# Background modulations of a two-layer decoder trunk: the sum over partitions with ones as weights, and a row that goes through DRAM

## The chip, the cores and the metric

The kernel runs on one core of one Trainium2 chip. The metric is the device time of one execution in microseconds (us): the median of three runs, with the lowest and the highest beside it. Engines are named as in the profile: PE is TensorE (PEld its weight loads), DVE is VectorE, ACT is ScalarE, POOL is GpSimd. SP only issues DMAs here, one after the other, and a DMA that has to wait holds back all that stand behind it on SP.

## The reference

The trunk has two layers of two sub-layers each, numbered j = 0 to 3 below: a gated spatial mixer (0), a squared-ReLU MLP (1), dilated attention (2) and a second MLP (3). Each sub-layer is modulated by one conditioning vector:

```python
def ada_mod(c, w, b):
    m = jax.nn.silu(c) @ w + b
    shift, scale, gate = jnp.split(m, 3, axis=-1)
    return shift[:, None, :], scale[:, None, :], 1.0 + gate[:, None, :]
...
for i in range(DEPTH):
    shift, scale, gate = ada_mod(c, ada_w[i, 0], ada_b[i, 0])
    h = x * (1.0 + scale) + shift
    y = mixer_a(h, ...) if i % 2 == 0 else mixer_b(h, ...)
    x = layer_norm(ALPHA * x + gate * y, ln_g[i, 0], ln_b[i, 0])
    shift, scale, gate = ada_mod(c, ada_w[i, 1], ada_b[i, 1])
    h = x * (1.0 + scale) + shift
    x = layer_norm(ALPHA * x + gate * squared_relu_mlp(h, ...), ln_g[i, 1], ln_b[i, 1])
```

x is 1024 rows of 1024 features, c one row of 1024, and each w is 1024 x 3072, all in float32. The change concerns `silu(c) @ w + b` alone: for each j three rows of 1024 numbers.

## The kernel before

All large products run on PE as three passes of a high and a low part ("hi" and "lo", made by `split`, L112: ACT copies, DVE subtracts). The work goes through the stages mixer (`mixer_a`), first MLP (`mlp(1)`), values, attention, second MLP (`mlp(3)`). A scheduler sets each engine's order from the order of the program and its own estimate of times; instructions marked `keep_in_program_order` stay where the program has them.

The modulations of j = 0 are made at the start. The others are **background work**: `ada_steps` (L133) cuts them into small steps, `later` (L199) puts the steps into one queue, and `tick` (L206) takes the next step from it at fixed places of the foreground: in the mixer two at a time or six per weight unit (L634, L661, L704), in the first half of an MLP one or two per product (L992). A group is one half row of 512 numbers (half h of part 0, shift, 1, scale, or 2, gate). Its steps are:

- eight steps (L142): load 128 x 512 of w (L145, tile `adaw`, four buffers), multiply by silu(c), which lies along the partitions, and add to the accumulator `adaacc` (DVE, L148 and L151). After eight steps the sum over the 128 partitions is still to be taken.
- `reduce` (L159): split `adaacc` into `adahi` and `adalo`.
- `total` (L168), held back until the third step of the next group is queued: the sum over partitions on PE. For a gate (part 2) the ones are the weights and the 512 columns stream past them (L173, L174), so that every partition of the bank `psa` holds the whole row; DVE adds 1 (L176) and one partition is written to `gate_dram` (L177). For shift and scale, which are needed with features along the partitions, `mod_cols` (L122) has the parts as weights, 128 columns at a time, and streams two columns of ones (L126, L127): eight weight loads and eight matmuls of 128x2. DVE adds the bias from the bank (L131). When both shift and scale of a half are there, three more DVE instructions (L185 to L187) fold them with the layer norm's weights into `mul` and `add`.

The banks of `psa` come from the PSUM pool `tr`, which has two buffers and also serves the mixer's transposes (`pszt`, L716). There are 12 groups of shift and scale in the background: four for j = 1 in the mixer, four for j = 2 and four for j = 3 in `mlp(1)`; and eight of gates.

In the mixer the names that matter are: `u_unit` (L694) with its weights `winu_hi` and `winu_lo` (units u0 to u7; four buffers each, so u4 takes the tile of u0) and its sums `psu`; `norm_v` (L673), one ACT and two DVE instructions (L676 to L678) per row tile of `vz`; `part_v` (L682) with `vhi` and `vlo`; `spatial` (L686), whose matmuls `psz` (L400) read them; and `gate_unit` (L709) with the transposes `pszt` (L716) that DVE reads (L719). In an MLP's first half `left` are the weights of the products `psua`, `psub`, `psuc` (L914), made five products ahead.

Of the kernel before, what the change touches and what calls it, by code (L numbers as in the profile page):

```python
# [10 lines left out]
F32 = mybir.dt.float32  # L11
F32R = mybir.dt.float32r
AF = mybir.ActivationFunctionType
ALU = mybir.AluOpType
# [3 lines left out]
P = 128  # L18
S = 1024
D = 1024  # L20
NT = S // P
KD = D // P
HALF = 512
# [12 lines left out]
def trunk(ctx: ExitStack, tc: tile.TileContext, x, c, ada_w, ada_b, ln_g, ln_b, a_w_in, a_b_in,  # L36
# [3 lines left out]
    nc = tc.nc  # L40
    V, A, G, T = nc.vector, nc.scalar, nc.gpsimd, nc.tensor

    def pool(stack, name, bufs, **kw):
        return stack.enter_context(tc.tile_pool(name=name, bufs=bufs, reuse_waits="tile", **kw))

    cst = pool(ctx, "cst", 1)
# [7 lines left out]
    dram = pool(ctx, "dram", 1, space=DRAM)  # L54
# [10 lines left out]
    ones_r = cst.tile([P, P], F32R, name="ones_r")  # L65
# [5 lines left out]
    cols_b = cols_c[:, KD : KD + 64]  # L71
# [20 lines left out]
    def g_col(j):  # L92
        return cols[:, o_g + j * KD : o_g + (j + 1) * KD]

    def b_col(j):
        return cols[:, o_b + j * KD : o_b + (j + 1) * KD]
# [7 lines left out]
    def bank(kind, name):  # L104
        return ps[kind].tile([P, HALF], F32, name=name, tag=kind)
# [6 lines left out]
    def split(hi, lo, src, hi_engine=A, lo_engine=V):  # L112

        first = A.copy(hi, src) if hi_engine is A else hi_engine.tensor_copy(hi, src)  # L114
        return first, lo_engine.tensor_tensor(lo, src, hi, op=ALU.subtract)  # L115


    ada = [dict() for _ in range(4)]
    ada_p = vec = None
    gate_dram = dram.tile([4, D], F32, name="gate_dram")  # L120

    def mod_cols(j, part, h, pst, hi, lo):  # L122

        for k in range(4):
            w = slice(k * P, (k + 1) * P)
            T.matmul(pst[:, 2 * k : 2 * k + 2], hi[:, w], ones_r[:, 0:2], start=True, stop=False)  # L126
            T.matmul(pst[:, 2 * k : 2 * k + 2], lo[:, w], ones_r[:, 0:2], start=False, stop=True)  # L127
        src = pst[:, 0:8].rearrange("p (k t) -> p k t", t=2)[:, :, 0]
        bias = cols_b[:, 16 * j + 8 * part + 4 * h : 16 * j + 8 * part + 4 * h + 4]
        res = ada[j][part, h] = cst.tile([P, 4], F32, name=f"ada_{j}_{part}_{h}")  # L130
        V.scalar_tensor_tensor(res[:], src, float(part), bias, ALU.add, ALU.add)  # L131

    def ada_steps(j, order, raw_bufs=2):  # L133


        i, s = divmod(j, 2)
        todo = []
        for part, h in order:
            box = {}
            w0 = part * D + h * HALF  # L140

            def step(k, part=part, h=h, box=box, w0=w0):  # L142
                nm = f"{j}_{part}_{h}"
                raw = ada_p.tile([P, HALF], F32, name=f"adaw_{nm}_{k}", tag="adaw", bufs=raw_bufs)
                nc.sync.dma_start(raw[:], ada_w[i, s, k * P : (k + 1) * P, w0 : w0 + HALF])  # L145
                if k == 0:
                    acc = box["acc"] = ada_p.tile([P, HALF], F32, name=f"adaacc_{nm}", tag=f"adaacc{part % 2}")
                    ins = V.tensor_scalar(acc[:], raw[:], silu_c[:, 0:1], None, ALU.mult)  # L148
                else:
                    acc = box["acc"]  # L150
                    ins = V.scalar_tensor_tensor(acc[:], raw[:], silu_c[:, k : k + 1], acc[:], ALU.mult, ALU.add)  # L151
                tc.keep_in_program_order(ins)

            def bias_row(part=part, h=h, box=box, w0=w0):
                if part == 2:
                    row = box["row"] = ada_p.tile([P, HALF], F32, name=f"adab_{j}_{h}", tag="adaw", bufs=raw_bufs)
                    nc.sync.dma_start(row[0:1, :], ada_b[i, s, w0 : w0 + HALF].unsqueeze(0))

            def reduce(part=part, h=h, box=box):  # L159
                nm = f"{j}_{part}_{h}"  # L160
                acc = box["acc"]
                hi, lo = (ada_p.tile([P, HALF], F32R, name=f"ada{m}_{nm}", tag=f"ada{m}") for m in ("hi", "lo"))
                if part == 2:
                    V.tensor_tensor(acc[0:1, :], acc[0:1, :], box["row"][0:1, :], op=ALU.add)
                split(hi[:], lo[:], acc[:])
                box["sum"] = (hi, lo)

            def total(part=part, h=h, box=box, w0=w0):  # L168
                nm = f"{j}_{part}_{h}"
                hi, lo = box["sum"]  # L170
                pst = bank("tr", f"psa_{nm}")
                if part == 2:
                    T.matmul(pst[:], ones_r[:], hi[:], start=True, stop=False)  # L173
                    T.matmul(pst[:], ones_r[:], lo[:], start=False, stop=True)  # L174
                    row = ada_p.tile([P, HALF], F32, name=f"gaterow_{nm}", tag="gaterow")
                    V.tensor_scalar(row[:], pst[:], 1.0, None, ALU.add)  # L176
                    nc.sync.dma_start(gate_dram[j, w0 - 2 * D : w0 - 2 * D + HALF].unsqueeze(0), row[0:1, :])  # L177
                    return
                mod_cols(j, part, h, pst, hi[:], lo[:])
                if (0, h) in ada[j] and (1, h) in ada[j]:  # L180
                    sh, sc = ada[j][0, h], ada[j][1, h]
                    mul = cst.tile([P, 4], F32, name=f"mul_{j}_{h}")
                    add = cst.tile([P, 4], F32, name=f"add_{j}_{h}")
                    o = slice(4 * h, 4 * h + 4)
                    V.tensor_tensor(mul[:], g_col(j - 1)[:, o], sc[:], op=ALU.mult)  # L185
                    V.tensor_tensor(add[:], b_col(j - 1)[:, o], sc[:], op=ALU.mult)
                    V.tensor_tensor(add[:], add[:], sh[:], op=ALU.add)  # L187
                    ada[j]["mul", h], ada[j]["add", h] = mul, add

            steps = [lambda k=k, step=step: step(k) for k in range(KD)]  # L190
            todo.append(steps[:-1] + [bias_row, steps[-1], reduce, total] if part == 2 else steps + [reduce, total])
        return todo

    GATE = ((2, 0), (2, 1))
# [2 lines left out]
    background = deque()  # L197

    def later(steps):  # L199
        held = []  # L200
        for group in steps:
            background.extend(group[:3] + held + group[3:-1])
            held = group[-1:]
        background.extend([lambda: None] * 3 + held)

    def tick(n=1):  # L206
        for _ in range(n):
# [271 lines left out]
    def mixer_a():  # L479
        nonlocal ada_p, vec  # L480
        with ExitStack() as ph:
# [147 lines left out]
            for i in range(6):  # L629
                v_end(0, i)  # L630
            later(ada_steps(0, GATE, 4) + ada_steps(1, MODS + GATE, 4))
            for n, _ in enumerate(in_turn((6, 2, range(KD)))):
                if n > 1:
# [150 lines left out]
    def mlp(j, before, ahead=iter(())):  # L784
# [5 lines left out]
        if j == 1:  # L790
            later(ada_steps(2, MODS + GATE, 4) + ada_steps(3, MODS, 4))
        else:
            later(ada_steps(3, GATE, 4))
# [1197 lines left out]
```

## Time and profile before

| | us |
|---|---|
| median of 3 runs | 2668.43 (2667.54 to 2671.32) |
| profiled execution, its time | 2666.83 |
| its span in the profile | 2665.1 |
| mixer, background of j = 1 | about 85 to 245 |
| first half of `mlp(1)`, background of j = 2 and 3 | about 330 to 648 |

The profiled execution is one run of the same kernel; its own time is 1.7 us above its span, and 1.6 us below the median. Busy times of an engine are sums over its instructions; the chain of waits follows the work that ended last back from the end, and what is not on it can be lengthened without effect until it gets onto it. In the rows of the chain an engine's matmuls are shown as a start, a length and a count.

### The profile page before, as it was taken

How to read it: one execution, taken by the hardware profiler on the slowest of the kernel's cores; microseconds unless marked ns; L12 is line 12 of the kernel's file. 1: busy time of each engine (PE TensorE's matmuls, PEld its weight loads, DVE VectorE, ACT ScalarE, POOL GpSimd, SP SyncE). 2: the span in 40 equal slices, each digit the busy share in tenths (PEclk: the TensorE clock that was granted, in tenths of full speed). 3: DMA queues.
4: the chain of work that ended last, by engine and by line, in shares of the span. 5: the costliest groups of instructions: out<-in, count | busy, mean ns of one | idle time of the engine just before them, and what ended most of it. 6: DMA issues, size and time to landing. Idle time of an engine off the chain costs nothing.

```text
span 2665.1 us, 36954 instructions
## 1 busy us (share of the span) xinstructions
PE 2639.0 (99%) x13204; PEld 2184.3 (82%) x13204; DVE 1978.8 (74%) x3548; ACT 1390.0 (52%) x2623; POOL 104.4 (4%) x189
## 2 busy tenths in 40 slices
PE   8999999999999999999999999999999999999998
PEld 6788888888888888888888888888888888888887
DVE  6895798886988888555557777777658965677887
ACT  4364475555444554333436666666656655554442
POOL 0000000000000001111110000000010000000000
PEclk9999999999999999999999999999999999999999
DMA  8643357677967646565565554454783654495562
GB/s 292 191 139 99 114 183 242 227 241 265 327 208 248 205 157 214 197 205 182 182 204 152 158 134 131 136 148 136 227 230 123 220 178 158 146 318 191 178 208 89
DMA packets 335068, 505.28 MB, mean 190 GB/s; under 512 B 51692, under 2 KB 168852, under 8 KB 334884
## 3 DMA queue, kind: packets, MB, share of 16 engines
q1 hardware_dynamic: 318500, 444.20, 52.6%
q0 software_dynamic: 16384, 58.73, 6.2%
q8 instruction: 103, 1.69, 0.3%
q14 instruction: 81, 0.66, 0.1%
HBM read 365.92 MB, written 136.92 MB: 189 GB/s over the span
## 4 chain that ended last, share of the span: by engine, by line
PE 94%; DVE 3%; DMA 1%; ACT 1%; issue 1%; SPq 0%; POOL 0%; DVEq 0%; ACTq 0%; POOLq 0%
PE psd L1081 23%; PE psua L914 13%; PE psv L1410 13%; PE psk L1511 7%; PE psuc L914 7%; PE psq L1511 7%; PE psd_wout L417 3%; PE psub L914 3%; PE pv L1684 3%; PE psv L513 3%; PE psu L701 3%; PE sc L1604 3%; PE pT L1657 1%; PE psoa L1888 1%; PE psoe L1888 1%; PE psod L1888 1%
## 5 line engine op out<-in xcount | busy, mean ns | idle before, releaser
L914 PE MATMUL psua<-right,left 128*128 128x512 f32 x1536 | 363.5, 390 | 0.1
L1081 PE MATMUL psd<-rhi,lhi 128*128 128x512 f32 x880 | 343.5, 390 | 0.0
L1081 PE MATMUL psd<-rlo,lhi 128*128 128x512 f32 x880 | 342.5, 389 | 0.0
L1081 PE MATMUL psd<-rhi,llo 128*128 128x512 f32 x880 | 342.5, 389 | 0.0
L914 PEld LDWEIGHTS psua<-right,left 128*128 128x128 f32 x1536 | 287.0, 188 | 61.3 <-DVE left L115 0.7
L1626 ACT ACTIVATE p<-p,stat 128x128 f32<-128x128 f32 (+1 forms) x384 | 168.7, 441 | 96.0 <-DVE stat L1624 92.6
L1081 PEld LDWEIGHTS psd<-rhi,lhi 128*128 128x128 f32 x880 | 165.2, 188 | 35.1 <-ACT part L945 0.9
L1081 PEld LDWEIGHTS psd<-rhi,llo 128*128 128x128 f32 x880 | 165.2, 188 | 34.6
L1081 PEld LDWEIGHTS psd<-rlo,lhi 128*128 128x128 f32 x880 | 165.2, 188 | 33.9
L914 PE MATMUL psuc<-right,left 128*128 128x512 f32 x768 | 187.2, 391 | 0.0
L914 PEld LDWEIGHTS psuc<-right,left 128*128 128x128 f32 x768 | 143.4, 188 | 30.4 <-DVE right L115 0.6
L115 DVE TENSOR_TENSOR pTlo<-pT,pThi 128x512 fp32r<-128x512 f32 (+1 forms) x160 | 99.3, 621 | 76.3 <-ACT pThi L114 75.3
L115 DVE TENSOR_TENSOR left<-ws,left 128x512 fp32r<-128x512 f32 x128 | 88.0, 689 | 81.0 <-ACT left L114 79.3
L115 DVE TENSOR_TENSOR llo<-lraw,lhi 128x1024 fp32r<-128x1024 f32 x112 | 136.5, 1221 | 2.3 <-ACT lhi L114 2.3
L1511 PE MATMUL psk<-form_L,wqk_hi 128*128 128x512 f32 x384 | 127.1, 412 | 0.0
L1511 PE MATMUL psq<-form_L,wqk_hi 128*128 128x512 f32 x384 | 126.5, 410 | 0.0
L114 ACT CAST lhi<-lraw 128x1024 fp32r<-128x1024 f32 x112 | 116.9, 1046 | 11.7 <-PE psd L1081 6.7
L1410 PE MATMUL psv<-vrhi,form_S 128*128 128x512 f32 x384 | 119.9, 390 | 1.4 <-DVE vpart L1376 0.9
L114 ACT CAST left<-ws 128x512 fp32r<-128x512 f32 x128 | 79.2, 620 | 78.1 <-DVE ws L838 67.6
L1624 DVE CUSTOM_DVE_ANT_0 p<-sc,bias 128x128 f32<-128x128 f32 (+1 forms) x384 | 113.8, 346 | 4.8 <-PE sc L1604 4.2
L114 ACT CAST pThi<-pT 128x512 fp32r<-128x512 f32 (+1 forms) x160 | 84.7, 530 | 61.6 <-PE pT L1657 44.8
L151 DVE SCALAR_TENSOR_TENSOR adaacc<-adaw,silu_c,adaacc 128x512 f32<-128x512 f32 x140 | 105.1, 751 | 5.6 <-DMA adaw<-in_ada_w_dram 4.9
(356 smaller groups left out, 6092.6 us busy)
## 6 DMA issues: line engine op xcount, KB each, us to landing
lraw<-forms SPq DMA_DIRECT2D x112, 512.0 KB
adaw<-in_ada_w_dram SPq DMA_DIRECT2D x160, 256.0 KB
up<-in_mlp_w_up_dram SPq DMA_DIRECT2D x64, 512.0 KB
forms<-s SPq DMA_DIRECT2D x128, 256.0 KB
rraw<-in_mlp_w_down_dram SPq DMA_DIRECT2D x64, 512.0 KB
forms<-part SPq DMA_DIRECT2D x96, 256.0 KB
v<-vs POOLq DMA_DIRECT2D x48, 512.0 KB, 3.7
vraw<-in_b_w_qkv_dram SPq DMA_DIRECT2D x42, 512.0 KB
```

What stands on the lines that cost most here:

```text
L114: first = A.copy(hi, src) if hi_engine is A else hi_engine.tensor_copy(hi, src)
L115: return first, lo_engine.tensor_tensor(lo, src, hi, op=ALU.subtract)
L151: ins = V.scalar_tensor_tensor(acc[:], raw[:], silu_c[:, k : k + 1], acc[:], ALU.mult, ALU.add)
L417: T.matmul(p[:], stat[a][:, k, o : o + P], u[b][:, w], start=n == 0, stop=n == count - 1)
L513: T.matmul(sums[i][:], hT[half][a_][:, k, o : o + P], units[c, k // 2][b_][:, n : n + HALF], start=k + a_ + b_ == 0, stop=k == KD - 1 and ...
L914: T.matmul(acc, w[:, a, k, :], right[p][:, b, k, :], start=p in (1, 2, 5) and k + a + b == 0, stop=k == 3 and a == 1, skip_group_check=True)
L1081: ins = T.matmul(sums[kind, m][:], l[a][:, k, m * P : (m + 1) * P], r[b][:, k, :], start=p in (1, 5, 2, 3) and kp + k + a + b == 0, stop=k ...
L1410: T.matmul(acc, rows[:, m * P : (m + 1) * P], cols_, start=p in (1, 2, 5) and kp + k + a + b == 0, stop=kp == 1 and k == 1 and a == 1, ski ...
L1511: T.matmul(p[:], wu[a][:, k * P : (k + 1) * P], h_op(k, half, b), start=k + c_ == 0, stop=k == KD - 1 and c_ == 2)
L1624: V.tensor_tensor_reduce(out=pr, in0=banks[e][:, sl], in1=st["bias"][:, width - w :], scale=-0.125, scalar=3e38, op0=ALU.add, op1=ALU.min, ...
L1626: A.activation(pr, pr, AF.Exp, bias=nm, scale=-1.0, accum_out=l)
L1888: T.matmul(sums[i, dh][:], ending["oT"][half][a][:, k, o : o + P], ending["units"][k][b][:, w], start=k == todo[0][0] and a + b == 0, stop ...
```

## The change

`mod_cols` goes. Shift and scale now take the gates' path on PE: the ones are the weights, and `adahi` and `adalo` stream past them as 128x512, two matmuls in place of eight. The row that results is copied by ACT from the bank to SBUF (`gaterow`), one partition of it is written to a new DRAM tensor `mod_dram` by SP, and a second DMA on SP (`fetch`) reads it back so that feature k*128+p lands on partition p: 128 partitions of four numbers each, each number a 4-byte piece of its own in DRAM. DVE then adds the bias in place in SBUF (`columns`), where it added it from the bank before. `mul` and `add` are folded as before, at the second of the two parts.

`later` spreads the three: `total` stands where it stood, `fetch` goes with the next step, `columns` three steps behind that. At the end of the queue seven empty steps stand in place of three. The lines below line 130 lie 10 lines lower in the changed file.

```diff
-    def mod_cols(j, part, h, pst, hi, lo):
-        for k in range(4):
-            w = slice(k * P, (k + 1) * P)
-            T.matmul(pst[:, 2 * k : 2 * k + 2], hi[:, w], ones_r[:, 0:2], start=True, stop=False)
-            T.matmul(pst[:, 2 * k : 2 * k + 2], lo[:, w], ones_r[:, 0:2], start=False, stop=True)
-        src = pst[:, 0:8].rearrange("p (k t) -> p k t", t=2)[:, :, 0]
...
-        V.scalar_tensor_tensor(res[:], src, float(part), bias, ALU.add, ALU.add)
+    mod_dram = dram.tile([4, 2, D], F32, name="mod_dram")
...
                 pst = bank("tr", f"psa_{nm}")
+                T.matmul(pst[:], ones_r[:], hi[:], start=True, stop=False)
+                T.matmul(pst[:], ones_r[:], lo[:], start=False, stop=True)
+                row = ada_p.tile([P, HALF], F32, name=f"gaterow_{nm}", tag="gaterow")
                 if part == 2:
...
                     return
-                mod_cols(j, part, h, pst, hi[:], lo[:])
-                if (0, h) in ada[j] and (1, h) in ada[j]:
+                A.copy(row[:], pst[:])
+                nc.sync.dma_start(mod_dram[j, part, h * HALF : (h + 1) * HALF].unsqueeze(0), row[0:1, :])
+
+            def fetch(part=part, h=h):
+                if part < 2:
+                    ada[j][part, h] = cst.tile([P, 4], F32, name=f"ada_{j}_{part}_{h}")
+                    nc.sync.dma_start(ada[j][part, h][:], mod_dram[j, part, h * HALF : (h + 1) * HALF].rearrange("(k p) -> p k", p=P))
+
+            def columns(part=part, h=h):
+                if part == 2:
+                    return
+                bias = cols_b[:, 16 * j + 8 * part + 4 * h : 16 * j + 8 * part + 4 * h + 4]
+                res = ada[j][part, h][:]
+                V.scalar_tensor_tensor(res, res, float(part), bias, ALU.add, ALU.add)
+                if part == 0:
                     sh, sc = ada[j][0, h], ada[j][1, h]
...
+        nothing = lambda: None
+        held = None
+        def also(f, g):
+            return lambda: (f(), g())
+        for body, ends in steps + [([nothing] * 7, None)]:
+            if held:
+                total, fetch, columns = held
+                body = body[:3] + [total, also(fetch, body[3])] + body[4:6] + [also(columns, body[6])] + body[7:]
+            held = ends
+            background.extend(body)
```

The scheduler places neighbouring work anew around these steps. Three places are shown, all in the mixer around the second of its four groups of shift and scale (`psa_0_0`, the shift's first half for j = 1).

On ACT, before, behind the square root `r_v` of the mixer's own layer norm (the eight `vz<-vz,mv_v` are the first halves of `norm_v`):

```order
L254 ACTIVATE r_v<-r_v 128x8
L676 ACTIVATE vz<-vz,mv_v 128x512 x8
L705 ACT_TABLE_LOAD
L705 ACTIVATE ut_1195<-psu_1_1233,cols 128x512
L705 ACTIVATE ut_1295<-psu_0_1296,cols 128x512
L676 ACTIVATE vz<-vz,mv_v 128x512 x4
L114 CAST vhi_1281<-vz 128x512
```

The same place on ACT in the change:

```order
L264 ACTIVATE r_v<-r_v 128x8
L114 CAST winu_hi<-winu_raw 128x1024
L686 ACTIVATE vz<-vz,mv_v 128x512 x8
L169 COPY gaterow_0_0_1263<-psa_0_0_1260 128x512
L715 ACT_TABLE_LOAD
L715 ACTIVATE ut_1194<-psu_1_1232,cols 128x512
L715 ACTIVATE ut_1286<-psu_0_1287,cols 128x512
L686 ACTIVATE vz<-vz,mv_v 128x512 x3
L715 ACTIVATE ut_1286<-psu_1_1328,cols 128x512
L114 CAST vhi_1272<-vz 128x512
```

Two instructions have come in ahead of the first `vhi`: the cast of the weights of unit u4 (before, it stood behind the `vhi` rows) and the new copy out of `psa_0_0`.

On DVE, before, the end of the same layer norm's statistics and the beginning of `norm_v`:

```order
L259 TENSOR_TENSOR mv_v<-r_v 128x8
L671 SCALAR_TENSOR_TENSOR mv_v<-mv_v 128x8
L677 TENSOR_TENSOR vz<-vz,vg 128x512
L678 TENSOR_TENSOR vz<-vz,vb 128x512
```

And in the change, from a little earlier (`adaacc_1_1` is the background sum that runs at the time):

```order
L141 SCALAR_TENSOR_TENSOR adaacc_1_1_1226<-adaw_1_1_4_1300,silu_c,adaacc_1_1_1226 128x512
L267 TENSOR_TENSOR r_v<-r_v 128x8
L141 SCALAR_TENSOR_TENSOR adaacc_1_1_1226<-adaw_1_1_5_1315,silu_c,adaacc_1_1_1226 128x512
L268 TENSOR_SCALAR r_v<-r_v 128x8
L269 TENSOR_TENSOR mv_v<-r_v 128x8
L681 SCALAR_TENSOR_TENSOR mv_v<-mv_v 128x8
L115 TENSOR_TENSOR winu_lo<-winu_raw,winu_hi 128x1024
L687 TENSOR_TENSOR vz<-vz,vg 128x512 x2
L688 TENSOR_TENSOR vz<-vz,vb 128x512 x2
```

Three more of the background's sums (k = 3, 4 and 5 of `adaacc_1_1`, the first of them a little above these rows) and the low part of unit u4's weights now stand ahead of the first `vz<-vz,vg`; before, the three stood behind it and u4's low part far behind.

On SP, in the change, the write of the row and the read back stand directly behind each other at this place:

```order
L395 DMA winu_raw<-in_a_w_in_dram 128x8x128
L170 DMA mod_dram<-gaterow_0_0_1263 1x512
L175 DMA ada_0_0_1266<-mod_dram 128x4x1
L135 DMA adaw_0_1_2_1427<-in_ada_w_dram 128x512
L135 DMA adaw_0_1_3_1452<-in_ada_w_dram 128x512
```

Before, loads of `adaw` stood there without a break. The read waits on SP until the write has landed, and the loads behind it with it. At other groups one to five DMAs stand between the two.

More of the change, by code (lines that the diff above doesn't have):

```diff
@@ L120, in trunk @@
     gate_dram = dram.tile([4, D], F32, name="gate_dram")
-    def mod_cols(j, part, h, pst, hi, lo):
-        for k in range(4):
-            w = slice(k * P, (k + 1) * P)
-            T.matmul(pst[:, 2 * k : 2 * k + 2], hi[:, w], ones_r[:, 0:2], start=True, stop=False)
-            T.matmul(pst[:, 2 * k : 2 * k + 2], lo[:, w], ones_r[:, 0:2], start=False, stop=True)
-        src = pst[:, 0:8].rearrange("p (k t) -> p k t", t=2)[:, :, 0]
-        bias = cols_b[:, 16 * j + 8 * part + 4 * h : 16 * j + 8 * part + 4 * h + 4]
-        res = ada[j][part, h] = cst.tile([P, 4], F32, name=f"ada_{j}_{part}_{h}")
-        V.scalar_tensor_tensor(res[:], src, float(part), bias, ALU.add, ALU.add)
+    mod_dram = dram.tile([4, 2, D], F32, name="mod_dram")
     def ada_steps(j, order, raw_bufs=2):
@@ L171, in total @@
                 pst = bank("tr", f"psa_{nm}")
+                T.matmul(pst[:], ones_r[:], hi[:], start=True, stop=False)
+                T.matmul(pst[:], ones_r[:], lo[:], start=False, stop=True)
+                row = ada_p.tile([P, HALF], F32, name=f"gaterow_{nm}", tag="gaterow")
                 if part == 2:
-                    T.matmul(pst[:], ones_r[:], hi[:], start=True, stop=False)
-                    T.matmul(pst[:], ones_r[:], lo[:], start=False, stop=True)
-                    row = ada_p.tile([P, HALF], F32, name=f"gaterow_{nm}", tag="gaterow")
                     V.tensor_scalar(row[:], pst[:], 1.0, None, ALU.add)
@@ L190, in ada_steps @@
             steps = [lambda k=k, step=step: step(k) for k in range(KD)]
-            todo.append(steps[:-1] + [bias_row, steps[-1], reduce, total] if part == 2 else steps + [reduce, total])
+            todo.append((steps[:-1] + [bias_row, steps[-1], reduce] if part == 2 else steps + [reduce], (total, fetch, columns)))
         return todo
@@ L199, in later @@
     def later(steps):
[L200 to L204, printed above, removed]
+        nothing = lambda: None
[8 more added lines that the diff above has]
+            background.extend(body)
     def tick(n=1):
```

## Prediction

> **What bounds the kernel now.** I read the page's first, second and fourth parts, then the chain of waits around the background groups, then the list of who waits for whom on PE.
>
> ```profile
> span 2665.1 us, 36954 instructions
> PE 2639.0 (99%) x13204; PEld 2184.3 (82%) x13204; DVE 1978.8 (74%) x3548; ACT 1390.0 (52%) x2623; POOL 104.4 (4%) x189
> PE 94%; DVE 3%; DMA 1%; ACT 1%; issue 1%; SPq 0%; POOL 0%; DVEq 0%; ACTq 0%; POOLq 0%
> PE pszt L716 <- DVE gaterow L176: 0.8, 1, 0.8
> ```
>
> PE is busy 99% of the span and carries 94% of the chain. So a microsecond of PE in the middle is a microsecond of the kernel, as long as nobody else becomes late. The last row is the only wait of PE, of those over 0.1 us, that lies between 95 and 640 us, where the change works: in the mixer a transpose waited 0.8 us for DVE to empty a bank (`tr`, two buffers).
>
> **What a group costs on PE, before and after.** In the chain, one group of shift or scale and one group of gates, both in `mlp(1)`, with the products around them:
>
> ```profile
> 402.53 0.00 PE psa L126
> 402.53 0.11 PE psa L127
> ...
> 403.20 0.11 PE psa L127
> 403.31 2.89 PE psuc L914 x12
> 406.20 5.44 PE psua L914 x24
> ...
> 504.27 0.24 PE psa L173
> 504.51 0.24 PE psa L174
> 504.75 5.49 PE psua L914 x24
> ```
>
> Eight small matmuls take 403.31 - 402.53 = 0.78, one weight load each 0.11. The product behind them takes 2.89, where twelve matmuls take 5.44 / 2 = 2.72: another 0.17, since its first weights could not be loaded under matmuls as short as these. Together 0.95. The gate group is the form that the change gives to all: 0.24 + 0.24, and 5.49 - 5.44 = 0.05 behind it: 0.53. So each of the 12 groups saves 0.42 on PE: 5.0 us in all, 1.7 in the four groups of the mixer and 3.4 in the eight of `mlp(1)`.
>
> The Trainium skill ("TensorE: Matmul & The Clock Gate", Back-to-back issue gap) gives about 131 ns per matmul of 512 columns in a sustained stream of weight loads and matmuls; by that the pair would cost 0.26 and the 12 groups would save some 7.7 us. The trace does not agree: 0.24 for each of exactly these matmuls, and 0.227 for the products, so the sum goes by 0.24.
>
> **`mlp(1)`: what the new steps do there.** Each group adds a copy of 128x512 out of PSUM on ACT, two DMAs on SP and a wait of SP for the first of them; DVE's bias addition stays what it was (0.16 before; I take the same). The nearest rows: a copy of that shape, the write of a gate's row, and attention's write of 16 KB to DRAM with the read that waits for it, once in quiet and once in a crowded stretch.
>
> ```profile
> 400.37 0.57 ACT L919 COPY part<-psua 128x512 f32<-128x512 f32 x1
> L177 SPq DMA_DIRECT2D gate_dram<-gaterow x8: 235/246/251, 94.2 to 2146.7; - x8
> 1456.38 0.34 SPq L1717 DMA_DIRECT2D st_dram<-statT  x1
> 1457.80 1.47 SPq L1739 DMA_DIRECT2D mst<-st_dram  x3
> DMA  0030000000000016841388125671000000000000
> 1977.23 1.52 SPq L1739 DMA_DIRECT2D mst<-st_dram  x3
> 1984.09 0.17 DVE L1748 TENSOR_TENSOR mm<-mm,mst 128x16 f32<-128x16 f32 x1 [2.02 <-DMA mst<-st_dram]
> ```
>
> From issue of the write to issue of the read: 1457.80 - 1456.38 = 1.42. The digits are the DMA view of 1457 to 1462 in slices of 0.125 us: the three reads, 512 pieces of 32 bytes each, move from 1458.75 to 1460.5, so the last of them ends 1.2 after SP has issued it (1457.80 + 1.47). I take 1.5 for the write and 2 for the read. The upper end is the crowded stretch: 1984.09 less 1978.75, 5.3 for the read. The lower end is nothing for either.
>
> The Trainium skill ("DMA: Bandwidth & Descriptors", Rules for kernel authors) speaks against this read: a strided last dimension lowers to one descriptor per element and should be rearranged to be contiguous. Here that is 512 descriptors of 4 bytes; by it the read costs as many pieces as one `mst` read, whose time stands above, and no run here shows pieces of 4 bytes.
>
> After `total`, then: copy 0.6, write 1.5, issue and read 2.4, so the columns are in SBUF some 4.5 us after the matmuls, 8 in a crowd. `columns` stands four ticks, about four products of 2.72 = 10.9, behind `total`, so DVE waits little or nothing. What would wait behind it is the weights of later products:
>
> ```profile
> 410.17 0.69 DVE L115 TENSOR_TENSOR left<-up,left 128x512 fp32r<-128x512 f32 x1
> 428.75 2.89 PE psua L914 x12
> 632.49 1.22 DVE L115 TENSOR_TENSOR llo<-lraw,lhi 128x1024 fp32r<-128x1024 f32 x1
> 641.03 0.69 DVE L838 TENSOR_TENSOR s<-part,s 128x512 f32<-128x512 f32 x1 [7.32 <-ACT part L923]
> ```
>
> The first weights of the next chunk are split at 410.2 and used at 428.75, 18 us later: that is the cover, and a DVE or SP that is 3 us late costs PE nothing. The last group meets the turn to the second half of the MLP; there `columns` falls into the 7.3 us in which DVE waited anyway. So `mlp(1)` gives its 3.4 us in full. Without the cover each group would cost what the wait exceeds it by.
>
> **The mixer: what is late next.** Here DVE is the second in line, and the new order costs it time (the three pieces shown above). The rows before:
>
> ```profile
> 125.00:165.00 40.00, 40.00 (x186) 33.31 (x185) 38.31 (x73) 28.07 (x41) 0.00 (x0) 1.00 0.45 135
> 134.70 1.22 DVE L115 TENSOR_TENSOR winu_lo<-winu_raw,winu_hi 128x1024 fp32r<-128x1024 f32 x1
> 138.52 5.76 ACT L676 ACTIVATE vz<-vz,mv_v 128x512 f32<-128x512 f32 x8 [1.64 <-DVE mv_v L671]
> 139.37 0.69 DVE L677 TENSOR_TENSOR vz<-vz,vg 128x512 f32<-128x512 f32 x1 [0.88 <-ACT vz L676]
> 140.07 0.00 PE psa L126
> 144.30 1.28 ACT L705 ACT_TABLE_LOAD   x1
> 147.08 2.92 ACT L676 ACTIVATE vz<-vz,mv_v 128x512 f32<-128x512 f32 x4
> 149.91 1.65 ACT L114 CAST vhi<-vz 128x512 fp32r<-128x512 f32 x3
> 150.59 1.29 DVE L115 TENSOR_TENSOR vlo<-vz,vhi 128x512 fp32r<-128x512 f32 x2
> 151.90 1.36 PE psz L400 x6
> 158.57 1.04 ACT L114 CAST winu_hi<-winu_raw 128x1024 fp32r<-128x1024 f32 x1
> ```
>
> DVE is busy 38.3 of 40 us there, and PE takes the products `psz` at 151.90, just when `vlo` is ready. In the change the cast of u4 (158.57 before) stands ahead of the eight `vz`. It takes the buffer of u0, so it waits until PE has finished u0: 140.07 before, 139.65 with one group's saving. It ends at 140.7, so the eight end 5.76 later at 146.5, where they ended at 144.3. Then the copy 0.57, the table load 1.28, two `ut` of 0.6 (as the copy), three `vz` of 0.73 (2.92 / 4) and a third `ut`: the first `vhi` starts at 152.4 and ends at 152.9; the first `vlo` ends 0.6 later, at 153.5. PE comes to `psz` at 151.90 - 0.84 = 151.06 and needs `vlo` third, at 151.5: it **waits about 2 us**. DVE by itself says nearly the same: u4's low part ends at 140.7 + 1.2 = 141.9, sixteen `vz` of 0.6 follow (a pair takes 1.29, one 0.69), then one more, `columns`, one more, and `vlo`: 153.3 to 153.9. Bounds: nothing, if the scheduler's order meets other times; 4.5, if the read takes 5.3. I take 2, since both engines give it. `columns` itself does not wait in this sum: the copy ends at 147.1, the read is issued at about 149.3 behind the write, the columns land at 151.3, and DVE comes to them at 152.2, 2.9 after the issue. Counted in the same way, DVE comes to the first sum 3.8 and to the fourth 4.8 us after the issue of their reads; at the third it is later still.
>
> Further on the mixer's end is set by DVE either way:
>
> ```profile
> 208.14 0.68 DVE adaacc L164
> 208.82 0.61 DVE gaterow L176
> 209.48 0.66 PE pszt L716 x4
> 210.14 1.16 PE psz L400 x5
> ```
>
> This is the wait of 0.8 from the first rows: PE went on at 209.48, when DVE had emptied the gate's bank. In the change PE comes here 2 - 1.7 = 0.3 to 0.5 us later than before, and DVE, whose amount of work up to here is the same, at 208.7 to 209.5. PE therefore leaves the place between 0.5 us earlier and 0.2 later than before. Had it not waited at `psz`, it would wait here. Of the mixer's 1.7 us I count 0.2.
>
> **The sum.** -3.4 in `mlp(1)`, -0.2 in the mixer: -3.6 us. Against the profiled execution's own 2666.83 that is 2663.2; the median of the runs shown, 2668.43, is 1.6 higher, which gives **2664.8**. Behind 650 us no wait of PE has to do with the change, and the gain is carried to the end. That is 0.13%, within the 0.2% (5.3 us) that a measurement of this kernel can tell from no change.
>
> **The rivals.**
>
> - *All of it arrives.* PE saves 5.0 and the wait of 0.8 goes as well: -5.8, 2662.6, faster by more than 0.2%. For it: no wait of PE in `mlp(1)`, and only one in the mixer. Against it: DVE would have to empty the gate's bank 2 us earlier with the same work. 0.14.
> - *The columns come late in the mixer.* With 5.3 us for the read, DVE stands at the first, second and fourth sum for 5.3 less 3.8, 2.9 and 4.8: 1.5, 2.4 and 0.5 us, and PE gets this at `psz` and `pszt`: -3.6 + 4.4 = 0.8, 2669.2. For it: 256 KB loads stand ahead of the read in the same queue. Against it: the DMA share there is 0.45, not that of the crowded stretch. 0.14.
> - *SP and DVE are held up, on the other side.* One mechanism: the read of 4-byte pieces is slow in itself. Every microsecond beyond the 3.8, 2.9 and 4.8 costs DVE, and PE behind it, one at each of these sums. The gain is used up at about 5 us a read, and 0.2% slower is reached at about 7. At 8 us it is 4.2 + 5.1 + 3.2 = 12.5: -3.6 + 12.5 = +9, 2677. Against it: 512 pieces in under 2 us in quiet. 0.10.
>
> **How the numbers follow.** Forecast 0.62, the rivals 0.14, 0.14 and 0.10. The range from 2661.5 to 2670 takes in the first two rivals and about 1 us of scatter, and leaves out the third. Faster by over 0.2%: the first rival and a little of the forecast's edge, 0.17; slower 0.10; within 0.2% the rest, 0.73.
>
> **What would show it.** In the changed profile: every group of `psa` in `mlp(1)` as two rows of 0.24 and a product behind it of 2.77; PE without a wait from 330 to 648; a PE wait of about 2 us at `psz` near 151, for `vlo` or `vhi`; the wait at `pszt` near 209 smaller than 0.8; the reads landing about 2 us after their issue and no DVE idle time put down to `ada<-mod_dram` worth more than 1 us. The forecast is wrong if PE waits at `psz` by 4 or not at all, if DVE stands at `columns`, or if a product in `mlp(1)` waits for its left weights.

## The result and the profile after

| | us |
|---|---|
| before, median of 20 runs beside the change | 2669.53 (2667.54 to 2672.45) |
| the change, median of 20 runs | 2666.03 (2663.21 to 2667.99) |
| ratio, 95% interval | 0.9986 (0.9979 to 0.9992) |
| profiled execution of the change: its time, its span | 2663.68, 2662.0 |

The change is faster by 0.14%, 3.5 us in the medians; between the two profiled executions the spans differ by 2665.1 - 2662.0 = 3.1. The forecast was 3.6 less, 2664.8 from a median of 2668.43; in this timing the kernel before took 1.1 us more than that.

The page's first part, and then the list of PE's waits between 90 and 330 us (between 330 and 650 there is none):

```profile
span 2662.0 us, 36882 instructions
PE 2634.6 (99%) x13132; PEld 2180.0 (82%) x13132; DVE 1977.6 (74%) x3548; ACT 1395.4 (52%) x2635; POOL 104.4 (4%) x189
```

```profile
PE psz L410 <- ACT vhi L114: 1.9, 1, 1.9
PE psa L162 <- ACT adahi L114: 0.5, 1, 0.5
```

PE has 72 instructions fewer (12 groups of 8 matmuls became 12 of 2) and 4.4 us less work, but the span is only 3.1 shorter: a wait of 1.9 at `psz` is new, and the 0.8 at `pszt` is gone. (The 0.5 at `psa` was there before.) Where the gain lies is read from marks on PE's timeline that both kernels have: the first `psu` of the mixer, the first transpose `pst` of the mixer's output stage, the first product `psua` of `mlp(1)` and the first `psd` of its second half. Of before, then of the change (start, length, engine, line, operation):

```profile
129.03 0.62 PE L701 MATMUL psu<-hT,winu_hi 128*128 128x512 f32 x2
...
308.54 0.60 PE L820 MATMUL pst<-ident,acc 128*128 128x128 f32 x4
...
330.01 2.91 PE L914 MATMUL psua<-right,left 128*128 128x512 f32 x12
...
647.70 0.39 PE L1081 MATMUL psd<-rhi,lhi 128*128 128x512 f32 x1
```

```profile
128.91 0.62 PE L711 MATMUL psu<-hT,winu_hi 128*128 128x512 f32 x2
...
153.24 1.02 PE L410 MATMUL psz<-vhi,wsT 128*128 128x512 f32 x2 [1.87 <-ACT vhi L114]
...
308.73 0.61 PE L830 MATMUL pst<-ident,acc 128*128 128x128 f32 x4
...
330.20 2.96 PE L924 MATMUL psua<-right,left 128*128 128x512 f32 x12
...
644.57 0.39 PE L1091 MATMUL psd<-rhi,lhi 128*128 128x512 f32 x1
```

From `psua` to `psd`: 647.70 - 330.01 = 317.69 before, 644.57 - 330.20 = 314.37 now, **3.32 less**. From `psu` to `pst`: 308.54 - 129.03 = 179.51 before, 308.73 - 128.91 = 179.82 now, **0.3 more**, although three groups of the mixer lie in that stretch (the first lies ahead of it) and the wait of 0.8 went. All of the gain is made in `mlp(1)`, as far as this pair of profiles shows. These two stretches are the measure of all experiments, since the work ahead of the mixer differs from execution to execution: the first `psu` came between 128.3 and 131.1 in the profiles of this study. e1 to e7, e11 and e12 below are one execution each, so only their stretches are read, not their times.

The page's fourth part gives PE 76% of the chain and "issue" 16% in this profile; in a second profile of the same kernel it is PE 93% and issue 1%. The chain had been followed back through attention by another way, so that change of shares means nothing here.

The groups in the chain, and DVE's two waits for a read (SP's issue of the read, then the instruction of DVE that waited; between square brackets the idle time and who ended it):

```profile
402.76 0.24 PE psa L162
403.00 0.24 PE psa L163
403.24 2.77 PE psuc L924 x12
```

```profile
125.61 0.24 SPq L170 DMA_DIRECT2D mod_dram<-gaterow  x1
...
127.75 0.38 SPq L175 DMA_DIRECT2D ada<-mod_dram  x1
```

```profile
131.11 0.16 DVE L182 SCALAR_TENSOR_TENSOR ada<-ada,cols_c 128x4 f32<-128x4 f32 x1 [0.79 <-DMA ada<-mod_dram]
...
635.13 0.16 DVE L182 SCALAR_TENSOR_TENSOR ada<-ada,cols_c 128x4 f32<-128x4 f32 x1 [4.26 <-DMA ada<-mod_dram]
...
637.90 0.69 DVE L848 TENSOR_TENSOR s<-part,s 128x512 f32<-128x512 f32 x1 [2.41 <-ACT part L933]
```

A group is 0.24 + 0.24 and a product of 2.77 behind it, 0.05 over 2.72: the 0.53 of the prediction. The first read of the mixer was issued at 127.75 and DVE went on at 131.11, so it took 3.4 at most; the last of `mlp(1)`, issued at 630.91, took 4.2, and there DVE stood 4.26 us without a wait of PE.

### The profile page after: what moved, and what is told of

Same layout as the page of the kernel before. It is cut to its first block, busy times and chain, and to the rows that moved or that the text cites. A ratio compares the mean times of both kernels' runs of the same rounds, so it can differ in the third digit from the quotient of the medians.

```text
span 2662.0 us, 36882 instructions
## 1 busy us (share of the span) xinstructions
PE 2634.6 (99%) x13132; PEld 2180.0 (82%) x13132; DVE 1977.6 (74%) x3548; ACT 1395.4 (52%) x2635; POOL 104.4 (4%) x189
## 4 chain that ended last, share of the span: by engine, by line
PE 76%; issue 16%; DVE 2%; POOL 2%; DMA 2%; ACT 1%; SPq 0%; POOLq 0%; DVEq 0%; ACTq 0%
PE psd L1091 20%; PE psua L924 13%; PE psk L1521 7%; PE psuc L924 7%; PE psq L1521 6%; PE psd_wout L427 3%; PE psub L924 3%; PE pv L1694 3%; PE sc L1614 3%; PE psu L711 2%; PE psv L523 2%; PE pT L1667 1%; POOL v L1397 1%; PE psoa L1898 1%; PE psoe L1898 1%
```

## Experiments: where the gain is made

The change was split by place. In the first kernel the mixer's four groups (j = 1) keep `mod_cols`, in the second the eight of `mlp(1)` (the same with `j > 1`). `mod_cols` is the one of before; its lines are left out here:

```diff
                 pst = bank("tr", f"psa_{nm}")
+                if part < 2 and j == 1:
+                    return mod_cols(j, part, h, pst, hi[:], lo[:])
                 T.matmul(pst[:], ones_r[:], hi[:], start=True, stop=False)
...
-                if part < 2:
+                if part < 2 and not j == 1:
                     ada[j][part, h] = cst.tile([P, 4], F32, name=f"ada_{j}_{part}_{h}")
...
-                if part == 2:
+                if part == 2 or j == 1:
                     return
```

> The new form in the eight groups of mlp(1) alone, the old mod_cols in the four groups of the mixer. Theory (the whole gain is the 0.42 us a group of mlp(1)): the mixer is as before, so PE does not wait at psz near 151, waits 0.8 at pszt near 209, the product psu behind it starts at 211.3 and the transposes of the output stage at 308.7; from there to the first psd of mlp(1) it is 3.3 to 3.4 us shorter than before (644.5 instead of 647.86). Span 2661.7. Rival (the mixer's groups give their 1.7 us too): with the old form there this kernel is 1.7 slower than the change, psd first at 646.4, span 2663.7.

> The new form in the four groups of the mixer alone, the old mod_cols in mlp(1). Theory: in the mixer PE waits 1.9 at psz near 151, not at pszt near 209, and leaves the mixer 0.2 later than before; mlp(1) as before, psd first at 648.1; span 2665.3, no gain. Rival (the mixer gives 1.7 us): psd first at 646.2, span 2663.4.

The marks of `mlp(1)` in the first kernel, then in the second:

```profile
329.52 2.93 PE L948 MATMUL psua<-right,left 128*128 128x512 f32 x12
...
643.84 0.39 PE L1115 MATMUL psd<-rhi,lhi 128*128 128x512 f32 x1
```

```profile
331.91 2.90 PE L948 MATMUL psua<-right,left 128*128 128x512 f32 x12
...
649.63 0.39 PE L1115 MATMUL psd<-rhi,lhi 128*128 128x512 f32 x1
```

The stretch of `mlp(1)` was 314.32 with the new form there and 317.72 with the old. In the mixer the first kernel had no wait at `psz`, 0.8 at `pszt`, and 179.37, as before; the second had 1.6 at `psz`, none at `pszt`, and 181.10. So the halves add up: the whole gain comes from `mlp(1)`, 3.3 to 3.4 for eight groups, and the mixer gives none. The second kernel was 1.5 slower in the mixer than expected. PE's rows behind the wait are longer there, and the windows of 1 us say why (length, busy times of PE, PEld, DVE, ACT and POOL, then the granted clock, the DMA share and GB/s):

```profile
152.00:153.00 1.00, 0.00 (x0) 0.00 (x0) 1.00 (x4) 1.00 (x3) 0.00 (x0) 1.00 0.00 0
...
154.00:155.00 1.00, 1.00 (x3) 0.88 (x4) 1.00 (x4) 0.89 (x2) 0.00 (x0) 0.57 0.00 0
155.00:156.00 1.00, 1.00 (x3) 0.74 (x3) 1.00 (x3) 0.59 (x1) 0.00 (x0) 0.50 0.00 0
156.00:157.00 1.00, 1.00 (x4) 0.78 (x3) 1.00 (x2) 0.41 (x2) 0.00 (x0) 0.50 0.41 137
157.00:158.00 1.00, 1.00 (x5) 0.83 (x4) 0.86 (x2) 1.00 (x3) 0.00 (x0) 0.73 0.54 176
```

Behind its idle time PE was granted half its clock for more than 3 us. From the first `psz` to the first `pszt` it took 168.16 - 153.38 = 14.78, where the change took 166.47 - 153.24 = 13.23 at a clock of 1.00: 1.55 more. Without that the stretch is 179.55. The wait can thus cost a second time, and does so in some executions.

## Experiments: what makes vhi late in the mixer

The scheduler's new order puts two things ahead of the eight `vz`: u4's cast on ACT, which the prediction named as the cause, and three sums `adaacc` on DVE, which it did not count. Each is held back by `behind` (L107), which keeps one instruction behind another in its engine's order. First the cast, behind the last of the eight:

```diff
         ins = split(hi, lo, raw, lo_engine=lo_engine)
+        if name == "winu_4":
+            behind(ins[0], marks["vz"])
```

> The change, but the cast of u4's weights on ACT is held behind the eight vz of the first half. Theory A (the cast is what makes the eight vz and so vhi late): the eight start before 140, vhi ends about 1.5 earlier, PE's wait at psz falls from 1.9 to 0.5 or less. Theory B (the statistics mv_v, which DVE ends at 141.17, are what the eight wait for; the cast ends at 140.82): the eight still start at about 141.2, PE waits 1.9 at psz, or up to 2.6 since two other instructions of ACT have moved to between the eight and vhi. Span 2662 to 2662.6 under B.

Then the sums, behind the last instruction of the statistics `mv_v` (mean and deviation of the layer norm, which the eight `vz` need as scale and bias):

```diff
+                if (j, part, h) == (1, 1, 1) and k > 2:
+                    behind(ins, marks["mv"])
                 tc.keep_in_program_order(ins)
```

> The change, but the three sums adaacc (features 3, 4, 5 of the mixer's third group) on DVE are held behind the statistics mv_v; the scheduler then puts u4's cast behind the eight vz by itself. Theory B: mv_v ends some 2 us earlier (three sums of 0.66), near 139.2, the eight start there, PE does not wait at psz near 151 (at most 0.3). Theory of the mixer's end (DVE empties the gate's bank near 209 whatever comes before): PE waits there about 2 us instead, psu behind it starts at 211.0 to 211.5, and the span is that of the change, 2661.5 to 2662.2. Rival (the wait at psz is the whole loss): no wait of that size at pszt, psu there at 209.6, span 2660.1.

With the cast held back PE waited longer, 2.7 at `psz` and 0.5 at `pszt`, and its clock fell behind the first wait (0.81 between 156 and 162): 182.69. Without the cast the eight `vz` still could not start before 140.98, when `mv_v` ended; they started at 141.25, behind a `ut` (the copy of a `psu` out of PSUM) that the scheduler had put in the cast's place. Later a second `ut` kept ACT waiting for PE for 1.19, which made `vhi` later still. With the sums held back the wait at `psz` was 0.3, at `pszt` 0.3, and the stretch 178.70. The eight started right behind `mv_v`:

```profile
140.63 0.17 DVE L684 SCALAR_TENSOR_TENSOR mv_v<-mv_v 128x8 f32<-128x8 f32 x1
140.83 5.76 ACT L689 ACTIVATE vz<-vz,mv_v 128x512 f32<-128x512 f32 x8 [2.44 <-DVE mv_v L684]
```

That is 140.83 - 130.54 = 10.29 after the first `psu`, where the change took 141.19 - 128.91 = 12.28. But in this kernel the scheduler also put u4's cast behind the eight, as the expectation had said, so e4 takes both out of the way. The last of the statistics before, then the change's own rows:

```profile
137.28 0.20 DVE L255 RECIPROCAL r_v<-r_v 128x8 f32<-128x8 f32 x1
...
138.32 0.17 DVE L671 SCALAR_TENSOR_TENSOR mv_v<-mv_v 128x8 f32<-128x8 f32 x1
```

```profile
138.29 0.19 DVE L265 RECIPROCAL r_v<-r_v 128x8 f32<-128x8 f32 x1
138.40 0.70 DVE L141 SCALAR_TENSOR_TENSOR adaacc<-adaw,silu_c,adaacc 128x512 f32<-128x512 f32 x1
139.02 0.16 DVE L266 TENSOR_TENSOR r_v<-r_v 128x8 f32<-128x8 f32 x1
139.13 0.75 DVE L141 SCALAR_TENSOR_TENSOR adaacc<-adaw,silu_c,adaacc 128x512 f32<-128x512 f32 x1
139.81 0.16 DVE L267 TENSOR_TENSOR r_v<-r_v 128x8 f32<-128x8 f32 x1
139.92 0.75 DVE L141 SCALAR_TENSOR_TENSOR adaacc<-adaw,silu_c,adaacc 128x512 f32<-128x512 f32 x1
...
140.99 0.17 DVE L681 SCALAR_TENSOR_TENSOR mv_v<-mv_v 128x8 f32<-128x8 f32 x1
```

```profile
139.77 1.05 ACT L114 CAST winu_hi<-winu_raw 128x1024 fp32r<-128x1024 f32 x1 [3.00 <-PE psu L711]
141.19 5.76 ACT L686 ACTIVATE vz<-vz,mv_v 128x512 f32<-128x512 f32 x8 [0.37 <-DVE mv_v L681]
```

Three sums sit between the links of a chain of small instructions that ends in `mv_v`, and each link waits for the sum ahead of it: from the first link shown to the end 141.16 - 138.29 = 2.87, where before took 138.49 - 137.28 = 1.21. The cast had ended at 140.82, only 0.37 before ACT started, and the row of the wait names DVE. In e2, e8 and e12, which have the same order, the cast ended about 0.1 before `mv_v`. So there are two limits almost at one place: holding the cast alone does not help (e3), and holding the sums alone, with the cast left where it is, could have brought the eight forward by 0.4 at most, by these rows. That kernel was not run. The e4 expectation was wrong in one point, though: it put some 2 us of wait at `pszt` in place of the wait at `psz`, and 0.3 came. DVE emptied the gate's bank 79.63 us after the first `psu`, 80.39 before: with `psz` in time, DVE too is earlier.

## Experiments: both limits of the mixer

The gate's bank is emptied by DVE between its sums. In the next kernel ACT does it for j = 1, on top of the edit of e4:

```diff
-                    V.tensor_scalar(row[:], pst[:], 1.0, None, ALU.add)
+                    if j == 1:
+                        A.activation(row[:], pst[:], AF.Identity, bias=one[:, 0:1])
+                    else:
+                        V.tensor_scalar(row[:], pst[:], 1.0, None, ALU.add)
```

> As e4_sums_back, and the two gate rows of the mixer (features of gates, part 2) are taken out of PSUM by ACT (the same 1.0 added) instead of DVE. Counted from the first psu of the mixer, since the time ahead of it differs by up to 1.6 us from run to run: to the first transpose of the output stage it was 179.51 before, 179.82 in the change, 178.70 in e4_sums_back. Theory (behind the wait at psz the next limit is DVE emptying the gate's bank, 0.34 in e4): that wait goes, 178.3, so the mixer gives 1.2 of its 1.7 us; no lowered clock. Rival (another wait takes its place): 178.7 or more, with a new row among PE's waits between 150 and 240.

The stretch was 178.27, with 0.4 at `psz` (for `vlo`) and nothing at `pszt`. As expected, but for the 0.4: three steps of that group still stood ahead of `mv_v`. Then all of that group's sums were held behind `mv_v` (and those of the mixer's later groups, which come behind it anyway); in e10 and e11 the bias additions `columns` were held by the same two lines, and there too the scheduler put u4's cast behind the eight `vz`:

```diff
+                if "mv" in marks and j == 1:
+                    behind(ins, marks["mv"])
                 tc.keep_in_program_order(ins)
```

with ACT taking the gate rows (e10, timed), with DVE taking them (e11), and with the change's order and ACT (e12):

> The change, with all sums of the mixer's third group on DVE held behind the statistics mv_v (five instead of three), and the mixer's gate rows taken out of PSUM by ACT as in e5. Theory: no wait of PE near 151 nor near 209; from the first psu to the first transpose of the output stage 179.51 before, less the wait of 0.84 and three groups of 0.42, 177.4 (the first of the four groups lies ahead of the first psu). With mlp(1)'s 3.4 and the first group's 0.42 that is 5.9 less than before: ratio 0.9978, 2663.6 where before takes 2669.5, 2.4 us ahead of the change. Rival (a third limit of DVE takes the place of the two): psu to output stage 178.3 or more as in e5, ratio 0.9982.

> As e10, but the gate rows stay on DVE as in the change: only the order ahead of the statistics mv_v is mended. Theory (the prediction's step: had PE not waited at psz, it would wait at pszt): no wait at psz near 151, 1.5 to 2.1 at pszt near 209 for gaterow, from the first psu to the output stage 178.9 to 179.6, where the change has 179.6 to 179.8 and e10 177.2. Rival (the order alone brings the gain of e10): no wait at pszt, 177.2.

> The change, and only the mixer's gate rows go to ACT. Theory (PE comes to pszt too late to wait there, so there is nothing to gain): 1.6 to 1.9 of wait at psz as in the change, none at pszt, from the first psu to the output stage 179.5 to 179.9 (1.5 more if the granted clock falls behind the wait). Rival (the gate rows on DVE cost the mixer anyway): 178.9 or less.

| first `psu` to `pst`, us (waits at `psz`, `pszt`) | gate rows by DVE | by ACT |
|---|---|---|
| order of the change | 179.82 (1.9, 0); again 179.59 (1.6, 0) | 179.49 (1.6, 0) |
| `mv_v` first | 178.40 (0, 1.0) | 177.18 (0, 0) |

PE's waits between 90 and 650 us in e10 and between 90 and 330 in e11:

```profile
PE psa L165 <- ACT adahi L114: 0.5, 1, 0.5
```

```profile
PE pszt L731 <- DVE gaterow L169: 1.0, 1, 1.0
PE psa L165 <- ACT adahi L114: 0.5, 1, 0.5
```

The gate rows alone bring nothing, since PE comes late to that place. The order (sums and cast) alone brings 1.2 to 1.4, less than the 2.4 to 2.6 of both, because a wait of 1.0 for the bank takes over; it was expected at 1.5 to 2.1, so DVE was thought later there than it is. Both together leave no wait, and the mixer gives 179.51 - 177.18 = 2.3, the first group's 0.42 beside it.

The timed runs, on one chip beside 24 runs of before (median 2668.63, 2666.36 to 2670.86):

> The changed kernel itself, timed beside the next two. Ratio to before 0.9986 as in its first timing (0.9979 to 0.9992). Theory of the clock (a wait of PE of 1.6 to 2.7 us near 151 lowers the granted clock to a half for some 3 us in some executions, worth 1.6 us, as in e2 and e3 and not in the first profile of this kernel): the profile shows a wait of 1.9 at psz with or without the low clock behind it; with it, the stretch from the first psu to the output stage is 181.4, without it 179.8.

> The kernel of e1 again, timed. Theory (the whole gain is made in mlp(1), and the mixer of before has no wait at psz): 3.4 less what before takes, ratio 0.9987, so 0.2 us ahead of the change where the clock stays, up to 1.6 more ahead of it where the clock falls behind the wait: between 0.2 and 1.8 us ahead of the change in the median. Rival (the mixer's groups bring their 1.7 us in the change): 1.7 behind it, ratio 0.9993.

| | median us | ratio, 95% interval |
|---|---|---|
| the change (e8) | 2664.59 (2662.53 to 2666.11) | 0.9984 (0.9976 to 0.9993) |
| new form in `mlp(1)` only (e9) | 2665.55 (2663.08 to 2667.07) | 0.9988 (0.9979 to 0.9998) |
| `mv_v` first, gate rows by ACT (e10) | 2661.98 (2660.11 to 2663.13) | 0.9974 (0.9964 to 0.9984) |

e10 takes less than both kernels: 6.7 us less than before, and 2.6 less than the change in the median, as its stretch says; the intervals of the two ratios still overlap. e9 was expected 0.2 to 1.8 ahead of the change and is 1.0 behind it, within the scatter. The timings thus give no sign that a low clock behind the wait at `psz` sets the change's median; its two profiles show 1.00 there. The mixer of e9 took 179.82, that of e1, the same kernel, 179.37: a stretch of the mixer is repeated to about 0.4 us, and the mixer's part of this change, +0.3 in one profile and +0.1 in the other, can't be told from nothing. The stretch of `mlp(1)` was between 314.29 and 314.37 in all eleven profiles with the new form there.

## Experiments: the reads, and the old form's price

To see whether the reads have cover, each was put off by two copies from DRAM to DRAM ahead of it. It was to become three times as long; from the issue of the first copy to DVE it came to 6.9 at the first read and 9.7 at the last, about twice the 3.4 and 4.2 of the change.

```diff
+                    nc.sync.dma_start(hop_dram[j, part, h * HALF : (h + 1) * HALF].unsqueeze(0), mod_dram[j, part, h * HALF : (h + 1) * HALF].unsqueeze(0))
+                    nc.sync.dma_start(hop2_dram[j, part, h * HALF : (h + 1) * HALF].unsqueeze(0), hop_dram[j, part, h * HALF : (h + 1) * HALF].unsqueeze(0))
-                    nc.sync.dma_start(ada[j][part, h][:], mod_dram[j, part, h * HALF : (h + 1) * HALF].rearrange("(k p) -> p k", p=P))
+                    nc.sync.dma_start(ada[j][part, h][:], hop2_dram[j, part, h * HALF : (h + 1) * HALF].rearrange("(k p) -> p k", p=P))
```

> The change, but each fetch goes from DRAM to DRAM twice before the read, so that the columns land some 10 us after the first of the three is issued (three times the 3.3 that the first read took). Theory (the cover): in mlp(1) DVE comes about 8 us after that, so it stands a few us at most columns, and PE does not notice: from the first psua to the first psd 314.4 as in the change (317.7 before). In the mixer there is no such cover: DVE stands at the first, second and fourth sum, 6.2, 7.1 and 5.2 at most by the counting of the prediction (10 less 3.8, 2.9, 4.8), less where the scheduler puts the sums later, and PE gets what DVE loses ahead of psz: from the first psu to the output stage 183 to 195 instead of 179.82. Rival (the cover isn't there): mlp(1) loses as well, several us in eight groups, 317 or more.

In `mlp(1)` nothing was lost: 314.29. DVE stood only 0.6 there, once, for the scheduler had put `columns` some 5 us later. In the mixer the expectation was far off: not 183 to 195 but 179.07, less than the change. The reason is in DVE's order: planned with later reads, the scheduler put the third group's sums behind `mv_v`, and u4's cast behind the eight `vz`. SP's issue of the first read, DVE's instruction behind it, the end of the statistics and PE's wait in this kernel:

```profile
131.74 0.39 SPq L179 DMA_DIRECT2D ada<-hop_dram  x1
...
133.86 0.16 DVE L186 SCALAR_TENSOR_TENSOR ada<-ada,cols_c 128x4 f32<-128x4 f32 x1 [0.64 <-DMA ada<-hop_dram]
...
136.22 0.17 DVE L685 SCALAR_TENSOR_TENSOR mv_v<-mv_v 128x8 f32<-128x8 f32 x1
```

```profile
PE pszt L730 <- DVE gaterow L168: 1.6, 1, 1.6
```

`mv_v` ended 136.39 - 128.32 = 8.1 after the first `psu`, in the change 141.16 - 128.91 = 12.25 after it. No wait at `psz`, and 1.6 at `pszt`. That is a second kernel in which the wait at `psz` goes with the order ahead of the eight `vz`, and the later reads did not bring it back; how much a read would cost that DVE meets at the same place, this run does not tell, since the scheduler moved the place. The rows also show the read with little beside it: from issue to DVE the 512 pieces of 4 bytes took 133.86 - 131.74 = 2.1 with a DMA share of 0.13 meanwhile, close to the 2 that the prediction took. In the change the share was 0.62 during the first read and 0.86 during the last.

The last run is about the old form's 0.95 a group: before, with 128 columns in each small matmul.

```diff
-            T.matmul(pst[:, 2 * k : 2 * k + 2], hi[:, w], ones_r[:, 0:2], start=True, stop=False)
-            T.matmul(pst[:, 2 * k : 2 * k + 2], lo[:, w], ones_r[:, 0:2], start=False, stop=True)
+            T.matmul(pst[:, P * k : P * (k + 1)], hi[:, w], ones_r[:, 0:P], start=True, stop=False)
+            T.matmul(pst[:, P * k : P * (k + 1)], lo[:, w], ones_r[:, 0:P], start=False, stop=True)
```

> The kernel before, with 128 columns instead of 2 in each of the eight small matmuls of a group (the same numbers in every column). Theory (each small matmul lasts as long as its own weight load, and the product behind the group starts 0.17 late because its first weights cannot be loaded under matmuls that are over at once): the eight still take 0.11 each, since 128 columns stream in about 0.06, and the product behind takes 2.83 to 2.85 instead of 2.89, as 0.06 of its load is now covered. Rival (the 0.17 is paid for the change between the two kinds of matmul): 2.89. If the columns add to the load instead, the eight take 0.16 each and a group 1.4.

```profile
402.88 0.06 PE psa L126
402.93 0.11 PE psa L127
...
403.61 0.11 PE psa L127
403.72 2.79 PE psuc L914 x12
```

Sixty-four times the columns, and the group costs less: 403.72 - 402.88 = 0.84 for the eight and 2.79 - 2.72 = 0.07 behind them, 0.91 in place of 0.95. The eight still come every 0.11, so it is not the columns that they last for; the first now shows the 0.06 that its columns take, and the product behind finds 0.10 more of its load covered, more than the 0.04 to 0.06 expected. A fixed price for the change of kind, 2.89, is refuted. The stretch agrees: 317.34, less than before by 0.35 for eight groups. (The mixer of this kernel took 180.26, with a wait of 1.3 at `pszt` in place of 0.8; why is not shown.)

## Why the prediction was right

- **What a group costs.** Right: 0.24, 0.24 and 2.77 in the chain, and 3.32 for eight groups where 3.4 was forecast; the eleven profiles with the new form in `mlp(1)` (314.29 to 314.37) and the two with the old one (317.69 and 317.72) repeat it. The sum that the prediction set beside it by the Trainium skill ("TensorE: Matmul & The Clock Gate", Back-to-back issue gap), 0.26 for the pair, is not borne out here: it is 0.48.
- **The round trip in `mlp(1)`.** The cover was right, PE has no wait from 330 to 648. The term for the read was mis-sized: 2 us were taken, 3.4 and 4.2 were measured where DVE waited, inside the bound of 5.3, and from write to read SP took 127.75 - 125.61 = 2.14 instead of 1.5. The sign "no idle time of DVE worth more than 1 us" failed with 4.26 at 635.13, and "if DVE stands at `columns`" was even named as a sign that the forecast is wrong. That was the group for which the prediction had named DVE's idle 7.3 us as cover, and it was: DVE waited 2.41 for ACT behind it and PE not at all. That sign was too strict; the step it stood for, that DVE's lateness there costs PE nothing, held. The rule on strided reads ("DMA: Bandwidth & Descriptors", Rules for kernel authors, of the Trainium skill) spoke against this read. Its price is not shown here: the same pieces took 2.1 in e6, so something besides the pieces made the change's reads longer, and no run has a contiguous read to compare.
- **The mixer: psz.** The wait came where it was forecast, 1.87 near 151.4 (2 at 151.1). Its cause was half of it: "the cast of u4" was to set the start of the eight `vz`, and in the change `mv_v` set it, held up by three sums that the change's order shows and the prediction did not count on this path. The cast ended only 0.4 earlier, so the sum came out right; for the size that is partly luck. e3 shows that the cast is not the only limit, e4 that the wait goes when sums and cast both stand behind. "`columns` itself does not wait" held but for 0.79 at the first group.
- **The mixer: pszt and the net.** That wait went, as forecast, and PE left the mixer 0.19 later in the two profiles' own times (the `psu` behind that place: 211.13 before, 211.32 in the change), at the edge of "0.5 earlier to 0.2 later"; -0.2 was counted. "Had it not waited at `psz`, it would wait here" is half right: e11 waits 1.0 there and still gains 1.2 to 1.4, since DVE comes earlier as well.
- **The sum.** 3.1 in the spans and 3.5 in the medians, 3.6 forecast.
- **The rivals.** *All of it arrives* did not come by itself. The reason given against it, DVE at the gate's bank, is 1.0 of that (e11); the wait at `psz` is the rest. With both limits lifted (e10) it came, 6.7 us by the medians where 5.8 was worked out. *Columns late in the mixer* and *slow reads* did not come: no read straight from `mod_dram` that DVE waited for took more than 632.20 - 627.65 = 4.6 (the last one, in e10), none in the mixer more than 3.4, and e6, with 2.1 for the read, speaks against "slow in itself". Their premise, that every microsecond of a late read reaches PE, was not tried with the order held.

## What to carry to other kernels

A gain on the busiest engine is worth what the stages it lies in let through: work it out for each stage, and look in each for the wait that comes next. When a scheduler places work anew around an edit, look for large background instructions between the links of a chain of small ones: here three such sums, of 0.66 us each, and a cast that had moved ahead with them took back what four groups had saved, and holding the sums behind the chain, with the gate rows moved to ACT, was worth 2.6 us where the change had brought 4.0. Where an edit lets the scheduler move a second suspect too, the run does not tell the two apart. Compare stretches between marks that both kernels have, not times from the start.

## What the runs showed of the hardware beyond that

- **The granted clock can halve behind a short wait.** After 1.62 us of waiting in e2 it was 0.50 from 154.2 to 157.5, which cost 1.55 us; after 2.69 in e3 it was 0.50 from 155.0 to 158.2. After 1.87 in the change, 1.64 in e8 and 1.65 in e12 it stayed at 1.00. Ahead of the mixer PE waits 0.66 and 0.92 between 65.5 and 67.5 in the change, 0.1 later in e4: in the change the clock stayed at 1.00, in e4 it was 0.50 from 68.3 to 71.6, one reason why the first `psu` moves. The Trainium skill ("TensorE: Matmul & The Clock Gate", What's actually happening) gives half the clock after an idle window of about 3.4 us, and calls the window free-running. The length of the slow stretch agrees with that; but here idle times of half that length were enough in some executions, and why not in others these runs do not show.
- **Matmuls with a weight load of their own came every 0.11 us with 128 columns as with 2** (e7), against 0.24 with 512 columns, where the ones are the weights; with 2 columns the product behind them took 0.17 longer, with 128 only 0.07.
